# Hybrid mLSTM and ConvFFN decoder layer: in the opening, the weight rows of the third to eighth row block are loaded into slots of their own, in two parts

## The chip, the core and the metric

The kernel runs on one core of one Trainium2 chip. The metric is device time in microseconds (us) for one execution; less is better. A kernel is run several times and the median is given. One more execution is recorded by the hardware profiler, and the views quoted below come from it. PE is the matrix engine (TensorE), DVE is VectorE, ACT is ScalarE, POOL is GpSimd, and SP is SyncE, which here only issues loads and stores. "SPq" and "ACTq" are instructions that issue transfers on the queues of SP and ACT.

## The reference: what is computed

One decoder layer in float32, for 512 positions of 1024 channels. A vector `c` makes six modulation vectors through one matrix, `ada_w` (1024 x 6144). The input `x` is normalised, scaled and shifted with the first two of them, and goes through one wide projection. Of its columns, four groups feed four mLSTM heads; the last 2048 are the two halves of a gated unit (GLU), which goes on into a causal convolution of width 31. Cut to what the opening computes:

```python
cond = jax.nn.silu(c)
mod = cond @ ada_w[l] + ada_b[l]
sh1, sc1, g1, sh2, sc2, g2 = jnp.split(mod[:, None, :], N_MOD, axis=-1)
u = rms_norm(x, mix_pre_g[l]) * (1.0 + sc1) + sh1
proj = u @ w_in[l]
...
a, gt = jnp.split(glu, 2, axis=-1)
y = causal_dwconv(a * jax.nn.sigmoid(gt), cv_dw_w[l], cv_dw_b[l])
```

After this come the heads, an output projection, a residual, and a ConvFFN with its own modulation and residual. None of that is touched by the change.

## The kernel before, in words

**The layout.** Activations stand with channels on the 128 partitions and the 512 positions along the free axis. The 1024 channels are eight row blocks, k = 0 to 7. Float32 products are made as three reduced-precision products: each operand is split into a high part (a rounded copy, made on ACT, line 191) and a low part (operand minus high part, made on POOL, line 192), and PE forms high x high, high x low and low x high.

**The opening (lines 269 to 422).** Six column tiles of the GLU (`G0 = 6`) are accumulated at once in six banks, so that PE can work on one row block k as soon as that block of `u` is there. For each k the steps are:

- `w_rows(k)` (lines 341 to 343) loads 128 rows of 768 weight columns, 384 KB, on SP's queue. The tile comes from the pool `adas`, which has two buffers (`ADAS = 2`), so block k uses the buffer of block k - 2.
- `first_load(k)` (lines 241 to 246) loads 1 MB of `ada_w`, in two halves of 512 KB, on SP's queue. Four such buffers exist (two of `raws`, two of `early`), so block k + 4 uses the buffer of block k.
- `part_sum(k, i)` (line 330) multiplies each half with the broadcast `silu(c)` on DVE and sums it; `part_gains` (lines 335, 336) turns the two sums into a scale and a shift for each channel.
- `w_part(k, ...)` splits the weight rows into high and low parts, first 512 columns and then 256 (lines 191 and 192: two instructions on ACT, two on POOL).
- ACT writes the high part of `u` (line 405) and a full copy (line 406), POOL the low part (line 407; DVE for k = 7).
- PE does 18 products of 128 x 128 by 128 x 512 (line 350): six banks, three products each.

**The order.** SP and PE run their instructions in the order of the program text. In iteration k, SP is given `w_rows(k + 1)`, then `first_load(k + 2)`; iteration 0 has `w_rows(0)` and `first_load(1)` ahead of these, and iteration 2 has one more load, the rest of the small vectors (line 363). After the opening SP goes on with the 1 MB weight loads of the other GLU tiles (line 199 by way of `glu_weights`). On ACT, DVE and POOL the instructions of the opening keep the order of the text among themselves (`in_order`, lines 76 to 88). Other instructions of those three engines are placed between them by a planner, which gives an engine the ready instruction of the highest priority; a lower priority is marked by `tc.cur_priority += LATER`.

**A later user of the same two buffers.** `ada_block(i)` (lines 168 to 178) loads 512 KB of `ada_w` for the later modulation vectors into a tile of the same pool `adas`, with an issue on ACT's queue (line 174). The blocks 16 to 19 (lines 895 to 898) are the first of these and are marked `LATER`; they are multiplied with `cb` on DVE (line 176), about 230 us after the opening.

**Completion counters.** In the program as it is built, each load or store takes one of eight completion counters, by turns, whichever engine issues it, and its instruction waits on the issuing engine until the transfer eight places before it has landed.

**The pool `slots`** has 36 buffers of 128 x 512 float32 (`SLOTS = 36`). In the opening before, 20 are taken: 2 by `crow`, 8 by `xn`, 2 by `xjunks`, 8 by `xr`.

Of the kernel before, what the change touches and what calls it, by code (L numbers as in the profile page):

```python
# [10 lines left out]
F32 = mybir.dt.float32  # L11
# [6 lines left out]
P = 128  # L18
D = 1024
T = 512  # L20
# [35 lines left out]
def decoder_layer(ctx, tc, w_glu0, x, c, adaT, vecs, w_glu, w_qko, w_v0, w_vo, w_out, w_up, w_down, out):  # L56
    nc = tc.nc
# [9 lines left out]
    adas = ctx.enter_context(tc.tile_pool(name="adas", bufs=ADAS))  # L67
# [22 lines left out]
    def slot(name, dt=F32):  # L90
        return slots.tile([P, T], dt, tag="t", name=name)
# [93 lines left out]
    def w_split(src, name, pool=None, tag="w", eng=None):  # L185

        n = src.shape[1]
        pool = pool or wpool
        hi = pool.tile([P, T], F32R, tag=tag, name=f"{name}h")
        lo = pool.tile([P, T], F32R, tag=tag, name=f"{name}l")  # L190
        S.activation(hi[:, :n], src, AF.Copy)  # L191
        (eng or G).tensor_tensor(out=lo[:, :n], in0=src, in1=hi[:, :n].bitcast(F32), op=ALU.subtract)  # L192
        return hi, lo
# [108 lines left out]
    def u_tiles(name):  # L302
        hi = upool.tile([P, KT, T], F32R, tag="uh", name=f"{name}h")
        lo = upool.tile([P, KT, T], F32R, tag="ul", name=f"{name}l")
        return hi, lo, [(hi[:, j, :], lo[:, j, :]) for j in range(KT)]

    _, _, u = u_tiles("u")
# [8 lines left out]
    G0 = 6  # L316
# [22 lines left out]
    rows0 = {}  # L339

    def w_rows(k):
        rows0[k] = adas.tile([P, D], F32, tag="ada", name=f"wglu0_{k}")
        nc.sync.dma_start(rows0[k][:, : G0 * P], w_glu0[k])

    def w_part(k, a, n):
        wk.append(w_split(rows0[k][:, a : a + n], f"wglu0_{k}_{a}"))

    def glu_pass(ps, i, p):
        a, b = ((0, 0), (1, 0), (0, 1))[p]
# [2 lines left out]
    for k in range(KT):  # L352
        wk = []

        if k == 0:
            w_rows(0)
            first_load(1)
        if k + 1 < KT:
            w_rows(k + 1)
# [4 lines left out]
        hi, lo = u[k]  # L364
        if k == 0:
            w_part(k, 0, T)
            part_sum(k, 0)
            part_sum(k, 1)
# [6 lines left out]
            V.tensor_scalar(out=xr[0], in0=xT_ps[0], scalar1=sc, scalar2=sh, op0=ALU.mult, op1=ALU.add)  # L375
            G.tensor_tensor(out=lo, in0=xr[k], in1=hi.bitcast(F32), op=ALU.subtract)
            w_part(k, T, (G0 - 4) * P)
            x_out(4, V)
            x_out(5, S)
            for i, p in ((0, 0), (1, 0), (0, 1), (1, 1), (2, 0), (2, 1), (3, 0), (3, 1)):  # L380
                glu_pass(banks0[i], i, p)
            for j in range(6, KT):
                for tt in range(NT):
                    turn_x(j, tt)
            wk, first_wk = [], wk
            w_part(1, 0, T)
            wk, next_wk = first_wk, wk
            x_out(6, S)
# [6 lines left out]
        else:  # L395
            if k == 1:
                wk = next_wk
# [690 lines left out]
    def conv3(ps, i, name):  # L1088
        t = cvtile(f"{name}c")
        w = lambda tap: vcol("ffn_conv_w", tap * 44 + i)  # L1090
        S.activation(t, ps, AF.Identity, bias=vcol("ffn_conv_b", i), scale=w(2))
        for d in range(1, 3):
            V.scalar_tensor_tensor(out=t[:, d:], in0=ps[:, : T - d], scalar=w(2 - d), in1=t[:, d:], op0=ALU.mult, op1=ALU.add)
        return t
# [39 lines left out]
    for i in range(NF):  # L1134
# [21 lines left out]
        a = conv3(pa, i, f"fa{i}")  # L1156
# [222 lines left out]
```

## Time and profile before

| | us |
|---|---|
| median of 3 runs | 768.84 |
| lowest and highest of them | 767.8 and 769.19 |
| the profiled execution, its own time | 769.16 |
| its span | 767.4 |
| PE busy in that span | 756.0 (99%) |
| the opening's last product on PE begins | 50.79 |

The profiled execution is 0.32 above the median, and 1.8 of its time lies outside the span. In the views, the first number of a timeline row is the start in us from the start of the span and the second is the duration; a row's bracket at the end gives the idle time of the engine before it and what ended that idle time. Consecutive instructions of one kind are merged into one row with their count (x4). "wglu" is the weight rows, "ada" the modulation weights, "uh" and "ul" the two parts of `u`; the index of the block is left out, and is found by counting. PE is never at a granted clock below 1.00 in the stage that the change touches, and its products come every 0.23 us when nothing holds them.

### The profile page before, as it was taken

Reading aid. Unit: us, or ns where it says so; the run is one execution under the profiler, and the core shown is the slowest. Engines: PE = TensorE matmul, PEld = TensorE weight load, DVE = VectorE, ACT = ScalarE, POOL = GpSimd, SP = SyncE. Lnnn points to the kernel's source line nnn. Section 1 sums busy time; section 2 is a strip of 40 time slices with the busy share of each in tenths; the row PEclk is TensorE's granted clock in tenths of the full one; section 3 lists DMA queues with packets and bytes.
Section 4 is the critical chain, followed back from the end, with each engine's and each line's share of the span. In section 5 each row is a group of like instructions: output and inputs, shape, how many; then the busy total and the mean of one; then the engine's idle time right before and its main releaser. Section 6 shows DMA issues by size and latency. Waiting matters only on the chain.

```text
span 767.4 us, 10129 instructions
## 1 busy us (share of the span) xinstructions
PE 756.0 (99%) x3480; PEld 625.1 (81%) x3480; DVE 576.6 (75%) x837; ACT 410.7 (54%) x778; POOL 516.5 (67%) x428
## 2 busy tenths in 40 slices
PE   7999999999999999999999999999999999999996
PEld 5778898878788788888889988888888888888885
DVE  6669999979979696476989978675684775654547
ACT  6675428585665655573345444443534444566633
POOL 4779849796494872645631179786887884599943
PEclk9999999999999999999999999999999999999999
DMA  8973313411131241655965755666767565796273
GB/s 317 349 281 113 112 56 117 158 56 56 55 111 56 98 168 64 235 199 168 365 222 183 271 210 191 240 219 247 262 231 275 187 239 185 271 397 241 93 249 135
DMA packets 40136, 147.32 MB, mean 192 GB/s; under 512 B 3826, under 2 KB 5266, under 8 KB 30484
## 3 DMA queue, kind: packets, MB, share of 16 engines
q1 hardware_dynamic: 27524, 96.59, 34.9%
q10 hardware_dynamic: 12560, 50.08, 18.3%
q8 instruction: 27, 0.44, 0.2%
q14 instruction: 25, 0.20, 0.1%
HBM read 126.59 MB, written 20.07 MB: 191 GB/s over the span
## 4 chain that ended last, share of the span: by engine, by line
PE 93%; DMA 4%; POOL 1%; ACT 1%; issue 0%; DVEq 0%; SPq 0%; DVE 0%; POOLq 0%; ACTq 0%
PE up L210 31%; PE dn L210 13%; PE qko L210 13%; PE vo L210 9%; PE glu L210 7%; PE mixa L210 6%; PE mixb L210 6%; DMA wglu<-in_w_glu 3%; PE o L562 2%; PE s L551 2%; PE v L210 2%; PE glu L350 1%; DMA xn<-in_x 1%; PE xT L992 0%; PE hT L593 0%
## 5 line engine op out<-in xcount | busy, mean ns | idle before, releaser
L774 DVE SCALAR_TENSOR_TENSOR cv<-gt,cvw,cv 128x485 f32<-128x485 f32 (+24 forms) x200 | 137.2, 731 | 2.1 <-ACT cv L762 0.8
L770 POOL TENSOR_TENSOR cs<-cs,cs 128x510 f32<-128x510 f32 (+3 forms) x32 | 42.1, 1316 | 0.2
L192 POOL TENSOR_TENSOR wup_0l<-wup,wup_0h 128x512 fp32r<-128x512 f32 x18 | 25.0, 1389 | 19.4 <-ACT wup_0h L191 19.3
L210 PE MATMUL up<-u2h,wup_0h 128*128 128x512 f32 (+1 forms) x96 | 35.8, 373 | 0.0
L210 PE MATMUL up<-u2h,wup_0l 128*128 128x512 f32 (+1 forms) x96 | 35.7, 371 | 0.0
L210 PE MATMUL up<-u2h,wup_512h 128*128 128x512 f32 (+1 forms) x96 | 35.6, 371 | 0.0
L210 PE MATMUL up<-u2l,wup_512h 128*128 128x512 f32 (+1 forms) x96 | 35.6, 371 | 0.0
L210 PE MATMUL up<-u2h,wup_512l 128*128 128x512 f32 (+1 forms) x96 | 35.6, 371 | 0.0
L210 PE MATMUL up<-u2l,wup_0h 128*128 128x512 f32 (+1 forms) x96 | 35.6, 371 | 0.0
L210 PE MATMUL up<-u2h,wup_1024h 128*128 128x512 f32 (+1 forms) x92 | 35.0, 381 | 0.0
L210 PE MATMUL up<-u2l,wup_1024h 128*128 128x512 f32 (+1 forms) x92 | 34.9, 380 | 0.0
L210 PE MATMUL up<-u2h,wup_1536l 128*128 128x512 f32 (+1 forms) x92 | 34.9, 380 | 0.0
L210 PE MATMUL up<-u2h,wup_1536h 128*128 128x512 f32 (+1 forms) x92 | 34.9, 380 | 0.0
L210 PE MATMUL up<-u2l,wup_1536h 128*128 128x512 f32 (+1 forms) x92 | 34.9, 380 | 0.0
L210 PE MATMUL up<-u2h,wup_1024l 128*128 128x512 f32 (+1 forms) x92 | 34.9, 380 | 0.0
L176 DVE SCALAR_TENSOR_TENSOR junk<-ada,cb 128x1024 bf16<-128x1024 f32 x20 | 29.9, 1493 | 2.6 <-DMA ada<-in_adaT 2.5
L768 ACT ACTIVATE cs<-gt,cvw 128x511 f32<-128x511 f32 (+4 forms) x40 | 27.1, 713 | 6.1 <-POOL cs L770 3.5
L192 POOL TENSOR_TENSOR wup_1536l<-wup,wup_1536h 128x512 fp32r<-128x512 f32 x18 | 24.6, 1365 | 6.0 <-ACT wup_1536h L191 5.4
L191 ACT ACTIVATE wup_512h<-wup 128x512 fp32r<-128x512 f32 x22 | 13.8, 629 | 25.7 <-PE up L210 20.9
L192 POOL TENSOR_TENSOR wup_1024l<-wup,wup_1024h 128x512 fp32r<-128x512 f32 x18 | 23.6, 1314 | 5.0 <-ACT wup_1024h L191 5.0
L330 DVE SCALAR_TENSOR_TENSOR junk<-ada,cps 128x1024 bf16<-128x1024 f32 x16 | 19.5, 1220 | 9.8 <-DMA ada<-in_adaT 9.2
L1113 DVE TENSOR_TENSOR b<-b 128x512 f32<-128x512 f32 x11 | 19.4, 1762 | 8.6 <-POOL b L1112 8.6
(1097 smaller groups left out, 2726.8 us busy)
## 6 DMA issues: line engine op xcount, KB each, us to landing
wup<-in_w_up SPq DMA_DIRECT2D x22, 1024.0 KB, 5.0
b<-in_w_down ACTq DMA_DIRECT2D x11, 1024.0 KB, 5.1
spill_t<-b ACTq DMA_DIRECT2D x11, 1024.0 KB, 3.9
ada<-in_adaT ACTq DMA_DIRECT2D x20, 512.0 KB, 4.8
wqko<-in_w_qko SPq DMA_DIRECT2D x9, 1024.0 KB, 4.8
ada<-in_adaT SPq DMA_DIRECT2D x16, 512.0 KB, 7.5
wo<-in_w_out SPq DMA_DIRECT2D x8, 1024.0 KB, 5.5
wvo<-in_w_vo SPq DMA_DIRECT2D x6, 1024.0 KB, 4.8
```

Of the source, the lines that this page charges most:

```text
L176: t = V.scalar_tensor_tensor(out=junk, in0=r, scalar=1.0, in1=cb, op0=ALU.mult, op1=ALU.mult, accum_out=mod[:, i : i + 1])
L191: S.activation(hi[:, :n], src, AF.Copy)
L192: (eng or G).tensor_tensor(out=lo[:, :n], in0=src, in1=hi[:, :n].bitcast(F32), op=ALU.subtract)
L210: PE.matmul(ps, l, r, start=start and i == 0, stop=stop and i == 2, skip_group_check=again)
L330: V.scalar_tensor_tensor(out=junk, in0=first[k][:, i * D : (i + 1) * D], scalar=1.0, in1=cps, op0=ALU.mult, op1=ALU.mult, accum_out=part[: ...
L350: PE.matmul(ps, blk(wk, i)[a], u[k][b], start=k == 0 and p == 0, stop=k == KT - 1 and p == 1)
L551: PE.matmul(sp[:, :n], ks[d][:, cc * P : (cc + 1) * P], qs[d][:, cc * P :], start=d == 0, stop=d == 1)
L562: PE.matmul(o[:, : DH + 2], E[h][cc][:, a : a + P], vs[h][cc], start=cc == 0, stop=cc == tt)
L768: S.activation(t[:, d:], cvx[j][:, : T - d], AF.Copy, scale=w(CK - 1 - d))
L770: G.tensor_tensor(out=side[:, d:], in0=side[:, d:], in1=t[:, d:], op=ALU.add)
L774: tap = V.scalar_tensor_tensor(out=cp[:, d:], in0=cvx[j][:, : T - d], scalar=w(CK - 1 - d), in1=cp[:, d:], op0=ALU.mult, op1=ALU.add)
L1113: V.tensor_tensor(out=b22, in0=b22, in1=b11, op=ALU.subtract)
```

## The change

For k = 0 and 1 nothing changes but how the two parts are named. For k = 2 to 7, the 768 columns go into two tiles of the pool `slots`, the first 512 columns into one and the other 256 into another, with one load for each. There is no tile of `adas` for these blocks any more. The split reads the part instead of a column range of one tile.

```diff
     def w_rows(k):
-        rows0[k] = adas.tile([P, D], F32, tag="ada", name=f"wglu0_{k}")
-        nc.sync.dma_start(rows0[k][:, : G0 * P], w_glu0[k])
+        if k < 2:
+            t = adas.tile([P, D], F32, tag="ada", name=f"wglu0_{k}")
+            nc.sync.dma_start(t[:, : G0 * P], w_glu0[k])
+            rows0[k] = t[:, :T], t[:, T : G0 * P]
+        else:
+            rows0[k] = slot(f"wglu0_{k}a"), slot(f"wglu0_{k}b")[:, : G0 * P - T]
+            for z, a in zip(rows0[k], (0, T)):
+                nc.sync.dma_start(z, w_glu0[k][:, a : a + z.shape[1]])
 
     def w_part(k, a, n):
-        wk.append(w_split(rows0[k][:, a : a + n], f"wglu0_{k}_{a}"))
+        wk.append(w_split(rows0[k][a // T], f"wglu0_{k}_{a}"))
```

Twelve tiles of `slots` and six more loads on SP's queue come of it; the bytes are the same, and the order of the loads in SP's text is the same.

## The prediction

> **What bounds the kernel now.** I read the page first, then PE's waits, then PE's own rows around the change.
>
> ```profile
> span 767.4 us, 10129 instructions
> PE 756.0 (99%) x3480; PEld 625.1 (81%) x3480; DVE 576.6 (75%) x837; ACT 410.7 (54%) x778; POOL 516.5 (67%) x428
> PE cps L159 <- ACT crow L158: 2.9, 1, 2.9
> PE glu L350 <- ACT uh L371: 1.3, 1, 1.3
> PE glu L350 <- ACT uh L405: 0.9, 1, 0.9
> ```
>
> PE is busy 99% of the span. The last three rows are all the waits of PE that the trace lists (total us, times, longest): nothing after the opening waits. So a product that starts earlier at the end of the opening should end the kernel earlier, and the change can give back only what PE loses in the opening from block 2 on. Those losses are in PE's rows; each row is the first group of a block (k = 1 to 7), the last one the first product behind the opening.
>
> ```profile
> 20.67 1.07 PE L350 MATMUL glu<-uh,wglu_0h 128*128 128x512 f32 x4
> 24.75 1.07 PE L350 MATMUL glu<-uh,wglu_0h 128*128 128x512 f32 x4
> 29.02 1.21 PE L350 MATMUL glu<-uh,wglu_0h 128*128 128x512 f32 x4
> 33.29 1.21 PE L350 MATMUL glu<-uh,wglu_0h 128*128 128x512 f32 x4
> 37.54 1.07 PE L350 MATMUL glu<-uh,wglu_0h 128*128 128x512 f32 x4
> 42.72 1.20 PE L350 MATMUL glu<-uh,wglu_0h 128*128 128x512 f32 x4 [0.94 <-ACT uh L405]
> 46.94 1.07 PE L350 MATMUL glu<-uh,wglu_0h 128*128 128x512 f32 x4
> 51.02 0.39 PE L210 MATMUL glu<-uh,wglu_0h 128*128 128x512 f32 x1
> ```
>
> Block 1 takes 24.75 - 20.67 = 4.08 us and shows no gap. Seven such blocks from 20.67 would end at 20.67 + 7 x 4.08 = 49.23; they end at 51.02. **The whole prize is 1.79 us**: 0.19 on blocks 2 and 3 each (4.27 - 4.08), 0.17 on block 4, 1.10 on block 5 (5.18 - 4.08), 0.14 on block 6.
>
> What ends these gaps is in ACT's rows: the start of the weight split of blocks 3, 4 and 6, with ACT's idle time before it.
>
> ```profile
> 27.32 0.63 ACT L191 ACTIVATE wglu_0h<-wglu 128x512 fp32r<-128x512 f32 x1 [3.03 <-DMA wglu<-in_w_glu]
> 31.59 0.63 ACT L191 ACTIVATE wglu_0h<-wglu 128x512 fp32r<-128x512 f32 x1 [1.77 <-DMA wglu<-in_w_glu]
> 41.03 0.63 ACT L191 ACTIVATE wglu_0h<-wglu 128x512 fp32r<-128x512 f32 x1 [3.41 <-DMA wglu<-in_w_glu]
> ```
>
> Each is followed by its block on PE 1.7 us later (27.32 to 29.02, 31.59 to 33.29, 41.03 to 42.72): two splits, then the high part of `u`, in ACT's fixed order. So the landing of the weight rows sets these blocks. Why they land late is in SP's rows and waits.
>
> ```profile
> 9.46 2.27 SPq L245 DMA_DIRECT2D ada<-in_adaT  x2
> 18.18 0.33 SPq L343 DMA_DIRECT2D wglu<-in_w_glu  x1
> SPq L343 <- POOL wglu_512l L192: 14.5, 6, 4.3
> SPq L245 <- DMA ada<-in_adaT: 1.3, 1, 1.3
> ```
>
> SP issues nothing from 11.73 to 18.18, and waits 14.5 us in six places for POOL's last split, which frees the `adas` buffer. The last row is the completion counters: the second half of the third `ada` block waits for the first half of the first, eight transfers before.
>
> The transfers themselves:
>
> ```profile
> 0.00:18.00 18.00, 13.84 (x62) 10.05 (x63) 11.09 (x31) 12.34 (x24) 8.25 (x21) 1.00 0.86 320
> 10.00:18.00 8.00, 6.69 (x45) 5.80 (x44) 6.67 (x14) 5.69 (x10) 4.30 (x6) 1.00 1.02 404
> 18.00:22.00 4.00, 4.00 (x21) 3.38 (x20) 3.96 (x10) 3.13 (x7) 2.99 (x4) 1.00 0.88 265
> 22.00:36.00 14.00, 13.97 (x61) 10.96 (x60) 8.39 (x19) 8.07 (x15) 10.36 (x11) 1.00 1.02 376
> 36.00:42.00 6.00, 5.78 (x26) 4.46 (x24) 3.04 (x8) 2.56 (x6) 3.27 (x4) 1.00 0.92 299
> 0.00:25.00 25.00, 20.84 (x95) 15.89 (x96) 16.38 (x42) 17.74 (x33) 14.19 (x27) 1.00 0.88 319
> 0.00:27.30 27.30, 23.14 (x105) 17.80 (x106) 17.92 (x46) 17.74 (x33) 14.94 (x27) 1.00 0.89 325
> ```
>
> The last two columns are the busy share of the transfer engines and GB/s. They run at 376 to 404 when fed, with dips to 265 and 299: the change can fill only these dips.
>
> **The change part by part.** *The removed waits.* SP no longer waits for POOL from block 2 on. Its next limits are the counters and the four `ada` buffers. By 18 us SP should have issued block 2's rows, `ada` 3 and block 3's rows, and the queue stays full. I place the landings by bytes, with these sizes:
>
> ```profile
> ada<-in_adaT SPq DMA_DIRECT2D x16, 512.0 KB, 7.5
> wglu<-in_w_glu SPq DMA_DIRECT2D x8, 384.0 KB, 6.7
> xn<-in_x SPq DMA_DIRECT2D x4, 256.0 KB, 4.3
> vec<-in_vecs SPq DMA_DIRECT2D x1, 296.0 KB
> ```
>
> At 18 us 320 x 18 = 5.76 MB have moved; `x` (eight of 256 KB, 2.10), `ada` 0 to 2 (3.15), two row blocks (0.79) and the first vectors (0.03) are 6.06, so 0.30 MB of `ada` 2 is left. Behind it, at 390 GB/s (the middle of 376 and 404), block 3's rows have moved at 18.0 + (0.30 + 0.39 + 1.05 + 0.39)/0.39 = 23.5, block 4's (with 1.05 of `ada` 4 and 0.30 of vectors) at 27.9, and then 1.44 MB or 3.7 us for each: 31.6, 35.4, 39.1. A landing lags behind this count: at 25.01 DVE begins on the second half of `ada` 3 when 319 x 25 = 7.98 MB have moved and 7.50 were needed (0.48 MB, 1.2 us), and at 27.32 ACT begins block 3's rows with 8.87 moved and 7.89 needed (0.98 MB, 2.5 us). So the lag is 1.2 to 2.5 us, I take 1.85. Block 3 lands at 25.4, its products could begin at 27.1, and PE is free at 24.75 + 4.08 = 28.83. Block 6: 37.2, 38.9, needed at 41.07. Block 7: 41.0, 42.7, needed at 45.15. The second landing that a block needs, its `ada`, is 0.39 MB ahead of the rows, and DVE needs 1.22 + 0.08 + 0.47 us behind it:
>
> ```profile
> L330 DVE SCALAR_TENSOR_TENSOR junk<-ada,cps 128x1024 bf16<-128x1024 f32 x11 | 13.4, 1222 | 8.9 <-DMA ada<-in_adaT 8.4
> ```
>
> that, too, is before PE asks. **So far: -1.79 us.**
>
> *Six more issues and smaller pieces.* 0.33 us each on SP, which has 14.5 us of waits to hide them; without that cover 6 x 0.33 = 2.0. How the transfer engines take a part of 256 columns, 1 KB a partition, no row of the opening shows. Lower end 0; upper end the spread of the fed rates above, 376 against 404, 7% of 2.4 MB, 0.4 us. Both lie inside the 1.7 us by which blocks 3 to 7 land early. I take 0.
>
> *Twelve tiles of `slots`.* 20 + 12 = 32 of 36, so none waits in the opening; the later users come when all twelve are read. 0.
>
> *The two buffers that become free.* This is the term that speaks against the change. The next users of `adas` are the `LATER` loads of `ada_block` 16 and 17.
>
> ```profile
> 42.70 0.81 ACT L406 ACTIVATE xr<-xr,gsk 128x512 f32<-128x512 f32 x1
> 43.01 0.74 POOL L192 TENSOR_TENSOR wglu_512l<-wglu,wglu_512h 128x256 fp32r<-128x256 f32 x1
> 43.79 0.33 ACTq L174 DMA_DIRECT2D ada<-in_adaT  x1
> 19.60 0.74 POOL L192 TENSOR_TENSOR wglu_512l<-wglu,wglu_512h 128x256 fp32r<-128x256 f32 x1 [0.20 <-ACT wglu_512h L191]
> ```
>
> Before, the first is issued at 43.79, 0.04 after POOL's split of block 6 frees the buffer (43.01 + 0.74), in the middle of ACT's opening work: the planner puts it as early as a buffer allows. After the change the buffers are free when block 0's and block 1's rows are split, by 18.18 (SP's row above waited for the first) and at 19.60 + 0.74 = 20.34, and nothing else takes them. So I expect 2 x 0.52 = 1.05 MB, not needed for 200 us, to enter the opening at 18 to 24 us on ACT's queue, between the transfers that PE waits for: 1.05/0.39 = 2.7 us. Block 3 then lands at 23.5 + 2.7 + 1.85 = 28.05, its products begin at 29.75 instead of 29.02; block 4 lands at 32.45, begins at 34.15 (PE would be free at 33.83); block 5 lands at 36.15, and from here PE asks later than the rows come: 34.15 + 4 x 4.08 = 50.47, against 51.02: **-0.55**. With the lag of 1.2 block 4 begins at 33.5, -1.2; with 2.5 at 34.8, +0.1; at 376 instead of 390 GB/s block 4 is 4.9 MB on and 0.5 later, +0.6.
>
> *ACT's queue.* The two issues also hold ACT, by the same counters: each waits until the transfer eight places before has landed. By the nearest row the hold is 0.28 (ACT is done at 42.70 + 0.81 = 43.51 and issues at 43.79), twice at most; by the far end it is a rival below. ACT has 4.08 - (0.63 + 0.40 + 0.80 + 0.82) = 1.4 us idle in a block, so most of it is hidden:
>
> ```profile
> 27.86 0.40 ACT L191 ACTIVATE wglu_512h<-wglu 128x256 fp32r<-128x256 f32 x1
> 28.17 0.80 ACT L405 ACTIVATE uh<-xr,gsk 128x512 fp32r<-128x512 f32 x1
> 29.00 0.82 ACT L406 ACTIVATE xr<-xr,gsk 128x512 f32<-128x512 f32 x1
> ```
>
> I take 0.15 on the path. **Sum: -0.55 + 0.15 = -0.4 us.** The profiled execution (769.16, span 767.4) lies 0.32 above the median; the difference is taken from the median, 768.84 - 0.4 = 768.4.
>
> The Trainium skill, "DMA: Bandwidth & Descriptors", section "Queues, rings and completion order", says that each transfer engine goes round the queues that have work and changes after a packet. By that rule the two loads on ACT's queue take half of each engine while they last, however much SP has queued, which is the delay of 2.7 us used above; if they stood behind SP's queue instead, the sum would be -1.8. No row here decides it: I found none where a load on ACT's queue had a long queue of SP's beside it.
>
> **The rivals.** *The full prize, 768.84 - 1.8 = 767.0.* The two loads come late, or the lag is short and they hide. For it: a slack of 1.7 us at block 3 without them. Against it: the 0.04 us of the row at 43.79.
>
> *ACT held, slower: about 770.3.*
>
> ```profile
> 20.27 0.82 ACT L406 ACTIVATE xr<-xr,gsk 128x512 f32<-128x512 f32 x1
> ```
>
> With the queue full, eight transfers are always on their way, and an ACT issue placed after block 1's work (ACT ends it at 20.27 + 0.82 = 21.1) waits for transfers that land at 24 to 27 us (`ada` 3 and block 3's rows, by the count above, with and without the 2.7). Behind it in ACT's order stand block 2's splits and its `u`; PE waits for them, and POOL for ACT. Block 2 then begins at 24.4 + 0.33 + 1.7 = 26.4 at the least and 29 at the most, not 24.75; from there PE needs 6 x 4.08 = 24.5 us, so the opening ends at 50.9 to 53.5: -0.1 to +2.5, middle +1.2, and with POOL's queue behind it I say +1.5. It decides from a hold of about 1.8 us (26.55 + 24.5 = 51.02). For it: 8 transfers are only about 2.8 MB, 7 us of work. Against it: ACT may issue while it waits for rows anyhow (the 3.03 and 1.77 us of idle time above).
>
> *Another order elsewhere.* The planner may place later work of DVE, ACT and POOL differently; PE has no listed wait there that could shrink, so this can only cost, some tenths: 769.
>
> **How the numbers follow.** Forecast 0.53, full prize 0.22, ACT held 0.20, another order 0.05. What a measurement of this kernel tells from no change is about 0.2%, 1.5 us. Faster by more: 0.7 of the full prize (its spread is -1.2 to -1.9) and 0.07 of the forecast, 0.15 + 0.04, and 0.02 for a gain that I don't see: 0.21. Slower by more: half of ACT held and 0.06 of the others: 0.14. Within: 0.65. The forecast's own range is -1.2 to +0.6, 767.6 to 769.4. The 8-in-10 range takes in the full prize, 766.9, and ACT held up to 770.2.
>
> **What would show it.** SP's rows for the weight rows of block 2 at 12 to 14 us, not 18.18; no wait of SP for POOL's split in the opening; two rows of ACT's queue for `ada` at 18 to 25 us, not from 43.79 on; the first product behind the opening (51.02 before) at 50.6, at 49.2 for the full prize, and past 51.5 for ACT held, with ACT idle before block 2's split. The gap of 1.10 us behind block 5 should be gone in either of the first two cases. Wrong is all of it if the time behind the opening changes by more than the opening does.

## The result, and the profile after

The changed kernel takes 770.3 us (median, 768.56 to 772.63) and the kernel before, on the same chip, 768.39 us (767.57 to 770.17). The ratio is 1.002, 95% interval 1.0014 to 1.0026: slower by about 1.5 us by the ratio and by 1.9 us by the medians, where no change was forecast. A few executions of these kernels took far longer than all others (up to 4382 us); the ratios leave them out, and one of them, at 1555.59 us, was the execution first profiled for the experiment e5_bytes_on_sp. The page of the kernel after begins so:

```profile
span 768.6 us, 10144 instructions
```

The difference lies in the opening. PE's rows in the timeline of the kernel after, the first group of each block (k = 1 to 6; block 7's is left out) and the first product behind the opening:

```profile
20.32 1.07 PE L356 MATMUL glu<-uh,wglu_0h 128*128 128x512 f32 x4
24.40 1.07 PE L356 MATMUL glu<-uh,wglu_0h 128*128 128x512 f32 x4
29.11 1.19 PE L356 MATMUL glu<-uh,wglu_0h 128*128 128x512 f32 x4 [0.47 <-ACT uh L411]
34.96 1.21 PE L356 MATMUL glu<-uh,wglu_0h 128*128 128x512 f32 x4 [1.46 <-ACT uh L411]
39.91 1.20 PE L356 MATMUL glu<-uh,wglu_0h 128*128 128x512 f32 x4 [0.54 <-ACT uh L411]
44.13 1.07 PE L356 MATMUL glu<-uh,wglu_0h 128*128 128x512 f32 x4
...
52.29 0.39 PE L210 MATMUL glu<-uh,wglu_0h 128*128 128x512 f32 x1
```

From block 1 to the first product behind the opening PE takes 52.29 - 20.32 = 31.97 us; before it took 51.02 - 20.67 = 30.35. What lies behind is the same: 768.6 - 52.29 = 716.3 us, before 767.4 - 51.02 = 716.4. The gap of 1.10 us behind block 5 is gone (44.13 - 39.91 = 4.22), and new ones stand before blocks 3, 4 and 5: 0.63, 1.77 and 0.87 us over the 4.08 of a block.

SP's own rows of the timeline, and its longest wait (total us, times, longest):

```profile
12.60 0.33 SPq L349 DMA_DIRECT2D wglu_2a<-in_w_glu  x1
...
18.31 0.33 SPq L349 DMA_DIRECT2D wglu_3a<-in_w_glu  x1
19.59 0.33 SPq L349 DMA_DIRECT2D wglu_3b<-in_w_glu  x1
26.14 0.80 SPq L245 DMA_DIRECT2D ada<-in_adaT  x2
...
28.66 0.90 SPq L245 DMA_DIRECT2D ada<-in_adaT  x2
SPq L245 <- DMA ada<-in_adaT: 13.1, 7, 6.1
```

SP never waits for POOL's split now. But between 19.92 and 26.14 it issues nothing: one wait of 6.1 us ahead of `ada` 4. ACT's rows:

```profile
17.86 0.33 ACTq L174 DMA_DIRECT2D ada<-in_adaT  x1
20.04 0.33 ACTq L174 DMA_DIRECT2D ada<-in_adaT  x1
...
27.12 0.63 ACT L191 ACTIVATE wglu_0h<-wglu_3a 128x512 fp32r<-128x512 f32 x1 [3.65 <-DMA wglu_3a<-in_w_glu]
...
33.13 0.63 ACT L191 ACTIVATE wglu_0h<-wglu_4a 128x512 fp32r<-128x512 f32 x1 [3.22 <-DMA wglu_4a<-in_w_glu]
```

The two loads of `ada_block` 16 and 17 went out at 17.86 and 20.04, and ACT was not held: its issues slip in between its other work. What it then waits for is weight rows. The windows of the kernel after (last two columns: busy share of the transfer engines, GB/s) show SP's queue running dry behind its wait (in 22 to 24 us they still moved 405 GB/s):

```profile
24.00:26.00 2.00, 2.00 (x11) 1.65 (x10) 1.54 (x4) 0.00 (x0) 1.33 (x2) 1.00 0.90 344
26.00:28.00 2.00, 2.00 (x10) 1.68 (x9) 0.00 (x0) 0.69 (x2) 0.17 (x1) 1.00 0.44 120
```

The chain that ended last, followed back from 54 us, names what SP waited for:

```profile
17.86 8.20 DMA ada<-in_adaT
...
26.08 0.02 SPq L245
...
29.12 8.25 DMA ada<-in_adaT
```

It is the load that **ACT** issued at 17.86. SP's first half of `ada` 4 is the transfer eight places behind it in the program's order (between them stand two parts each of the rows of blocks 2 and 3, the two halves of `ada` 3, and the second early load), so both use the same completion counter, and SP's issue waits until `ada_block` 16, which nobody needs for 200 us, has landed 8.20 us after its issue. By then SP is late with everything: it issues `ada` 4, the vectors, block 4's rows, `ada` 5 and block 5's rows in 4.4 us (26.14 to 30.57), and the second half of `ada` 5, issued at 29.12, lands only 8.25 us later and sets block 5.

### The profile page after: what moved, and what is told of

It is laid out like the page before. It is cut to its first block, busy times and chain, and to the rows that moved or that the text cites. A ratio compares the mean times of both kernels' runs of the same rounds, so it can differ in the third digit from the quotient of the medians.

```text
span 768.6 us, 10144 instructions
## 1 busy us (share of the span) xinstructions
PE 755.7 (98%) x3480; PEld 624.9 (81%) x3480; DVE 578.5 (75%) x837; ACT 412.1 (54%) x778; POOL 517.9 (67%) x428
## 4 chain that ended last, share of the span: by engine, by line
PE 94%; DMA 4%; SPq 1%; issue 0%; ACT 0%; DVE 0%; DVEq 0%; POOLq 0%; POOL 0%; ACTq 0%
PE up L210 31%; PE dn L210 13%; PE qko L210 13%; PE vo L210 9%; PE glu L210 7%; PE mixa L210 6%; PE mixb L210 6%; PE o L568 2%; PE s L557 2%; DMA ada<-in_adaT 2%; PE glu L356 2%; PE v L210 1%; DMA wglu<-in_w_glu 1%; DMA xn<-in_x 1%; PE hT L599 0%; PE xT L998 0%
## 5 line engine op out<-in xcount | busy, mean ns | idle before, releaser
L191 ACT ACTIVATE wup_512h<-wup 128x512 fp32r<-128x512 f32 x22 | 13.8, 629 | 26.7 <-PE up L210 20.2
```

## The experiments

My theory after this: the early loads cost in two ways, by holding SP through the counter and by their own 1.05 MB. The rivals: that the bytes alone do it; that loading in two parts, or from slots, does it; that ACT is held. All ratios are against the kernel before, with 95% intervals. "Opening" is the time from block 1's first product to the first product behind the opening; seven blocks without a gap are 7 x 4.08 = 28.56 us.

**The change without its early loads (e1_pin).** The two loads are put back behind the end of the opening on ACT, everything else is as changed (`behind_ins` keeps an instruction behind another one on the same engine):

```diff
-        nc.scalar.dma_start(r, adaT[i // 2][...])
+        load = nc.scalar.dma_start(r, adaT[i // 2][...])
+        if i < 18:
+            behind_ins(load, opened[0])
...
-    S.activation(cb, cps, AF.Copy)
+    opened.append(S.activation(cb, cps, AF.Copy))
```

> The changed kernel, with the loads of ada_block 16 and 17 queued on ACT behind the copy that ends the opening, so that they can't enter it. Theory (the loss comes from these two loads: the first takes a completion counter, lands after 8.2 us, and SP's issue of ada 4 waits for it until 26.14): without them SP isn't held, the first product behind the opening comes at 49.2 to 49.8 instead of 52.29, and the time is 1.2 to 1.8 us below the kernel before (ratio 0.9977 to 0.9984). Rival (the six more loads use up the eight counters, so that SP runs dry anyway): SP still shows a wait of several us for an ada landing, the first product at 51 or later, ratio 1.000 to 1.002. Rival (another order of later work): the opening is as in the theory, and the total doesn't follow it.

767.49 us, ratio 0.9992 (0.9983 to 1.0). SP's row of `ada` 4 and PE's first and last rows of the opening:

```profile
18.28 1.55 SPq L251 DMA_DIRECT2D ada<-in_adaT  x2
20.23 1.07 PE L362 MATMUL glu<-uh,wglu_0h 128*128 128x512 f32 x4
48.79 0.39 PE L216 MATMUL glu<-uh,wglu_0h 128*128 128x512 f32 x1
```

`ada` 4 goes out 7.86 us earlier. 2.65 of these were lost ahead of the long wait: block 3's second part leaves SP at 16.94 here and left it at 19.59 in the changed kernel, where the two early loads stand in two of the eight places. The transfers stay at 395 to 414 GB/s from 18 to 42 us, and the opening is 48.79 - 20.23 = 28.56 us: no gap at all. So all that the change loses, it loses by the two early loads; slots and two parts in themselves are no loss. The time gained less than I expected, 0.6 us by the ratio in place of 1.2 to 1.8, with an interval that reaches 1. And in this profile, at a mean granted clock of 0.949, the stretch behind the opening took 766.8 - 48.79 = 718.0 us, not 716.3.

**The same once more (e1_again)**, run beside e5 and the changed kernel's second measurement:

> e1_pin once more, for a second profile and a narrower interval. Theory: the opening without a gap on PE again, seven blocks of 4.08 us; the time behind the first product after the opening as in the kernels before and after, 716.3 to 716.5 us, where the first profile of e1_pin had 718.0 at a granted clock of 0.95; ratio to before 0.9985 to 0.9995. Rival (the pinned loads cost 1.6 us behind the opening): 718.0 again.

767.48 us, ratio 0.9986 (0.9978 to 0.9995). Again no gap, and behind the opening 767.6 - 51.33 = 716.3 us: the 718.0 belonged to that one execution, not to the loads put back. But in the profiled execution block 1 began 2.5 us later:

```profile
22.77 1.07 PE L362 MATMUL glu<-uh,wglu_0h 128*128 128x512 f32 x4
51.33 0.39 PE L216 MATMUL glu<-uh,wglu_0h 128*128 128x512 f32 x1
10.00:18.00 8.00, 5.62 (x34) 4.38 (x34) 6.86 (x14) 5.72 (x11) 4.56 (x6) 0.89 1.02 406
18.00:22.00 4.00, 4.00 (x20) 3.25 (x19) 3.93 (x9) 2.41 (x5) 2.31 (x4) 0.80 1.03 396
```

The granted clock (third number from the end) was 0.89 and 0.80 in these windows.

**The split alone (e2_split_only).** The kernel before, with the rows of blocks 2 to 7 loaded in two parts into the same buffers:

```diff
-        nc.sync.dma_start(rows0[k][:, : G0 * P], w_glu0[k])
+        for a, b in ((0, G0 * P),) if k < 2 else ((0, T), (T, G0 * P)):
+            nc.sync.dma_start(rows0[k][:, a:b], w_glu0[k][:, a:b])
```

> The kernel before, with only one part of the change: the rows of blocks 2 to 7 are loaded in two parts, but still into the two buffers by turns. Theory: SP is paced by the buffers, the six more issues hide in its waits for POOL, and the time is that of before within 0.3 us (ratio 0.9996 to 1.0004). Rival (the two parts cost counters): 0.5 to 1.5 us slower (1.0007 to 1.002), with waits of SP for ada landings in place of those for POOL.

768.42 us, ratio 1.0006 (0.9998 to 1.0015): no difference that this measures. The interval takes in both what I expected and values of the rival, so the time doesn't decide between them; e1, which has the same two parts and no gap, does. SP still waits 11.5 us for POOL:

```profile
SPq L344 <- POOL wglu_512l L192: 11.5, 6, 4.3
```

**The place in the order, without the bytes (e3_small_early).** As changed, but only the first 32 columns (16 KB) of each of the two loads go early; the rest follows behind the opening. The counters are taken as in the change.

```diff
-        nc.scalar.dma_start(r, adaT[i // 2][...])
+        cut = 32 if i < 18 else 0
+        if cut:
+            nc.scalar.dma_start(r[:, :cut], adaT[i // 2][...])
+        load = nc.scalar.dma_start(r[:, cut:], adaT[i // 2][...])
+        if i < 18:
+            behind_ins(load, opened[0])
...
```

> As the changed kernel, but of the loads of ada_block 16 and 17 only the first 32 columns (16 KB each) are loaded where the changed kernel has the whole, and the rest behind the opening: the same counters are taken at the same places of the order, without the 1 MB. Theory (it is the late landing of the big load on ACT's queue that holds SP): the small load lands 3 to 4 us after its issue, SP issues ada 4 by 22, and the time is that of e1_pin within 0.4 us. Rival (that any load of ACT stands in the row of counters is enough): SP is held as in the changed kernel, and the ratio to before is 1.001 to 1.002.

768.95 us, ratio 1.001 (1.0001 to 1.0019). From the timeline and the windows:

```profile
17.93 0.33 ACTq L180 DMA_DIRECT2D ada<-in_adaT  x1
18.39 0.33 SPq L358 DMA_DIRECT2D wglu_3a<-in_w_glu  x1
23.66 1.52 SPq L254 DMA_DIRECT2D ada<-in_adaT  x2
24.10 0.63 ACT L200 ACTIVATE wglu_0h<-wglu_3a 128x512 fp32r<-128x512 f32 x1 [0.58 <-DMA wglu_3a<-in_w_glu]
22.00:26.00 4.00, 4.00 (x19) 3.34 (x18) 2.77 (x6) 3.33 (x6) 4.00 (x5) 1.00 0.73 213
```

With 16 KB in place of 512 SP's `ada` 4 is still held until 23.66, 5.4 us later than in e1_pin, and the queue runs dry (213 GB/s). In the chain that ended last, ACT's load of 16 KB, from 17.93 on, is what SP's issue waited for: it lands 23.66 - 17.93 = 5.7 us after its issue, as long as the 256 KB that SP queued beside it (24.10 - 18.39 = 5.7). I had expected 3 to 4 us and the time of e1_pin; the rival's ratio came. So the hold needs the place, not the bytes; the bytes prolong the wait itself from 3.6 to 6.1 us, and the delay of `ada` 4 against e1_pin from 5.4 to 7.9. The opening here was 49.89 - 20.40 = 29.49 us, 0.93 over e1_pin, and by the medians the small loads cost 768.95 - 767.49 = 1.5 us against e1_pin, beside which they ran.

**The bytes, without the place (e5_bytes_on_sp).** As changed, with the two loads put into SP's own order, one behind `ada` 4 and the vectors, one behind `ada` 5 (there they take places in the round too, but ACT issues none of them):

```diff
...
+        if k in (2, 3):
+            i = 14 + k
+            ahead[i] = adas.tile([P, D], F32, tag="ada", name=f"ada_{i}")
+            nc.sync.dma_start(ahead[i], adaT[i // 2][...])
```

> The changed kernel, with the loads of ada_block 16 and 17 issued by SP in its own order, behind the vectors of block 2 and behind ada 5: the same 1.05 MB in the opening, but no load on ACT's queue. Theory (most of the loss is the late landing on ACT's queue under a counter that SP waits for, the bytes alone cost little): the transfers stay at about 400 GB/s, the opening ends up to 1 us later than in e1_pin, ratio to before 0.999 to 1.0005. Rival (the bytes are the loss): the opening ends 2.5 to 3.5 us later than in e1_pin, ratio 1.0015 to 1.0025.

768.04 us, ratio 0.9997 (0.9988 to 1.0007). Its profile is from one more execution:

> The kernel of e5_bytes_on_sp once more, for a profile with PE at its usual clock. If the bytes alone cost, as the times say (0.6 us over e1_pin): SP's ada 4 at 18.1, the queue at 395 to 405 GB/s through 18 to 40 us, and gaps of PE of some tenths before blocks 3 to 5, 1 us in all at most, with the opening from block 1's first product to the first behind block 7 at 28.6 to 29.6 us. If the loads stall something as in the changed kernel: a wait of SP over 5 us and an opening over 30.5.

767.74 us. ACT's start on block 4's rows, and the only gap for which the trace lists a wait of PE (0.67 us over the 4.08 of a block):

```profile
30.74 0.63 ACT L192 ACTIVATE wglu_0h<-wglu_4a 128x512 fp32r<-128x512 f32 x1 [4.20 <-DMA wglu_4a<-in_w_glu]
37.37 1.19 PE L357 MATMUL glu<-uh,wglu_0h 128*128 128x512 f32 x4 [0.49 <-ACT uh L416]
```

SP is on time (`ada` 4 at 18.38), the queue stays at 388 to 409 GB/s, and the opening is 49.75 - 20.37 = 29.38 us, 0.82 over e1_pin. The 1.05 MB alone cost that much in the trace and 768.04 - 767.48 = 0.56 us by the medians, against e1_again, beside which they ran, though the intervals of the two ratios overlap.

**The two loads on ACT's queue, at another place in the order (e7_behind_block2).** They stand behind block 2's `xr`:

```diff
-        nc.scalar.dma_start(r, adaT[i // 2][...])
+        load = nc.scalar.dma_start(r, adaT[i // 2][...])
+        if i in (16, 17):
+            behind_ins(load, opened[2])
...
-            S.activation(xr[k], xr[k], AF.Identity, scale=sc, bias=sh)
+            opened[k] = S.activation(xr[k], xr[k], AF.Identity, scale=sc, bias=sh)
```

> The changed kernel, with the two loads of ada_block 16 and 17 queued on ACT behind block 2's xr (which ends at about 23.4 us in e1_pin) in place of 17.9 and 20.0 us; nothing else moved. The place in the round of eight counters moves with them: now SP's issues of block 6's rows (29.34 in e1_pin) and of ada 7 (31.05) come eight places behind the two loads and have to wait for their landings. Theory 'the order of issue decides': SP's ada 4 goes out at 18.3 us, as in e1_pin; the two loads land some 5.7 to 8.2 us after 23.5, at 29.2 to 32; block 6's rows leave SP at up to 32, 2.7 late, but PE asks for block 6 only at 40.6, so that delay is hidden. What is left is the transfer of the 1.05 MB itself (e5_bytes_on_sp: 0.6 us over e1_pin): 767.5 to 768.3, 1.5 to 2.5 below the changed kernel, and not one wait of SP longer than 3 us before 28 us. Rival 'early bytes cost wherever they stand in the opening': 769.3 or more, near the changed kernel. Rival 'ACT held' (of the prediction): ACT waits at its issue for block 3's rows and ada 3 to land, block 3's split starts a microsecond or more late (23.80 in e1_pin), PE has a gap before block 3 or 4, 768.5 to 769.5.

769.17 us, ratio 1.0013 (1.0004 to 1.0021): above what my theory gave (767.5 to 768.3), just below what its first rival gave (769.3), and inside what the second, *ACT held*, gave (768.5 to 769.5). From the timeline:

```profile
23.27 1.99 ACTq L178 DMA_DIRECT2D ada<-in_adaT  x2
25.31 0.63 ACT L197 ACTIVATE wglu_0h<-wglu_3a 128x512 fp32r<-128x512 f32 x1 [1.81 <-issue]
32.06 0.63 ACT L197 ACTIVATE wglu_0h<-wglu_4a 128x512 fp32r<-128x512 f32 x1 [4.25 <-DMA wglu_4a<-in_w_glu]
33.75 1.19 PE L362 MATMUL glu<-uh,wglu_0h 128*128 128x512 f32 x4 [0.99 <-ACT uh L417]
```

SP's `ada` 4 is on time (18.37), as the theory had it, and the queue stays full (394 to 403 GB/s from 24 to 30 us). But the two loads now come between block 4's rows and their transfer. ACT began these rows at 29.35 in e1_pin, at 30.74 in e5_again and at 32.06 here. With 0.39 MB per us, one load of 0.52 MB ahead of them is 1.34 us and two are 2.69: 1.39 and 2.71 were measured. In e1_pin block 4 had 1.4 us to spare (29.35 + 1.7 = 31.05, and PE began it at 32.47); here PE waits 1.15 us for it (33.75 - 28.52 - 4.08). ACT, too, is held here, 1.81 us of idle time at its own issues, and block 3's split comes 1.5 us later than in e1_pin (23.80), hidden behind PE's work on block 2. So the signs that the second rival named are all there (the hold, the late split, a gap before block 4), but its cause isn't: ACT was free again 4.25 us before it could begin block 4, and waited for these rows. The opening is 50.72 - 20.36 = 30.36 us, 1.80 over e1_pin. Behind it the profile has 767.9 - 50.72 = 717.2 us in place of 716.3, of which 0.6 is one wait of PE between 120 and 140 us that no other profile has. So what my theory had left out is that a load on the second queue takes transfer time from rows that are already queued on the first: the order of issue alone doesn't decide.

**The same aim without free buffers (e4_sides).** The kernel before, with the rows of blocks 2 to 5 loaded by one transfer each into the halves of two `side` tiles and those of 6 and 7 in `adas`. So nobody becomes free to load early:

```diff
-        rows0[k] = adas.tile([P, D], F32, tag="ada", name=f"wglu0_{k}")
+        if 2 <= k < 6:
+            if k % 2 == 0:
+                wide0.append(side(f"wglu0_{k}"))
+            rows0[k] = wide0[-1][:, k % 2 * D : (k % 2 + 1) * D]
+        else:
+            rows0[k] = adas.tile([P, D], F32, tag="ada", name=f"wglu0_{k}")
```

> The kernel before, with the rows of blocks 2 to 5 each by one load into halves of the two wide side buffers, which nothing uses until the opening ends, and blocks 6 and 7 in the two buffers of before: no wait for POOL, no load in two parts, and the two buffers don't come free before 43 us, so ada_block 16 and 17 stay behind. Theory: as e1_pin, 1.2 to 1.8 us below before (ratio 0.9977 to 0.9984), within 0.3 us of e1_pin. Rival (the parts cost counters): clearly better than e1_pin, by over 0.5 us. Rival (the prize isn't there): 1.000.

767.34 us, ratio 0.9989 (0.9981 to 0.9998): 0.85 us below the kernel before by the ratio, where 1.2 to 1.8 were expected. The loads of `ada_block` 16 and 17 stay where they were, and there is no gap:

```profile
21.89 1.07 PE L355 MATMUL glu<-uh,wglu_0h 128*128 128x512 f32 x4
50.45 0.39 PE L210 MATMUL glu<-uh,wglu_0h 128*128 128x512 f32 x1
39.72 0.33 ACTq L174 DMA_DIRECT2D ada<-in_adaT  x1
```

50.45 - 21.89 = 28.56 us. It is, with e1, the fastest version found; both are a little faster than the kernel before.

**Both kernels again.** The changed kernel:

> The changed kernel once more, on the chip of e5. Theory (SP held by the counter of the first early load): SP again issues nothing for about 6 us before ada 4, at 26 us within 0.7, the first product behind the opening at 52.0 to 52.6, ratio to before 1.001 to 1.003. Rival (the hold was one execution's accident): the hold under 3 us in this one, the product before 51.

769.8 us, ratio 1.0016 (1.0007 to 1.0025). SP's `ada` 4 went out at 25.38, behind a wait of 5.2 us, with ACT's two loads at 19.01 and 21.56. Block 1 began late in this execution, and yet the opening ended where it had ended in the first profile of this kernel:

```profile
22.10 1.07 PE L356 MATMUL glu<-uh,wglu_0h 128*128 128x512 f32 x4
52.19 0.39 PE L210 MATMUL glu<-uh,wglu_0h 128*128 128x512 f32 x1
```

Counted from block 1 this opening is 52.19 - 22.10 = 30.09 us, no longer than those of the kernel before. For the time it is the end of the opening that counts: 52.29 and 52.19 here, 50.43 to 51.02 in three profiles of the kernel before.

The kernel before:

> The kernel before, a second profile of it. Theory: the profile that the prediction was worked from is of an execution about 1 us slower than the median, and the 1.10 us on PE behind block 5 is its own: here the opening from block 1 takes 29.2 to 29.8 us instead of 30.35. Rival: 30.2 to 30.5 again, and the gap behind block 5 with it.

> The kernel before once more, to see how long its opening usually is: from block 1's first product to the first behind block 7 it took 30.35 us in the execution shown and 29.90 in before_again; gap-free it is 28.56. If 30.35 is usual, 30.2 to 30.5 again and a gap of about 1.1 behind block 5; if the execution shown was a slow one, 29.4 to 30.0 and that gap 0.7 or less.

768.58 and 768.89 us, with openings of 29.90 us (20.53 to 50.43) and 30.56 us (20.20 to 50.76). In the last, the gap behind block 5 is again 42.45 - 37.30 - 4.08 = 1.07 us:

```profile
37.30 1.07 PE L350 MATMUL glu<-uh,wglu_0h 128*128 128x512 f32 x4
42.45 1.20 PE L350 MATMUL glu<-uh,wglu_0h 128*128 128x512 f32 x4 [0.92 <-ACT uh L405]
```

So the opening shown before the change, 30.35 us, was not an unusually long one among the three, against what I had come to think.

## Why the prediction was wrong

The forecast was 768.4 us, in effect no change; the result is 770.3 us, a small loss, outside the stated range of 766.9 to 770.2. Step by step:

*The removed waits: right.* SP's block 2 rows went out at 12.60 us, and no wait for POOL's split is left.

*The whole prize of 1.79 us: right in the trace, too large in the time.* Three profiles of the kernel before show openings 1.3 to 2.0 us longer than the gap-free 28.56, and e1 and e4 take all of that away. Yet by the ratios they are only 0.6 and 1.1 us (e1, twice) and 0.85 us (e4) below the kernel before. A part of the reason: with no gap left, the end of the opening moves with block 1's start one for one (20.23 to 48.79 and 22.77 to 51.33 in e1), while where transfers set the end it doesn't move (20.32 to 52.29 and 22.10 to 52.19 in the changed kernel). An execution with a late block 1, at a lower granted clock, thus takes the prize away. No profile of the kernel before shows such an execution, but the recorded runs, each with its mean granted clock, fit: at 0.995 and 0.996 those of e1 and e4 (7 of 33, median 768.8) are 0.3 us below those of the kernel before beside them (7 of 60, 769.1), and above that 1.0 us (767.2 against 768.1). Even there it is 1.0 and not 1.79, and why stays open. One estimate: in ten of the twelve profiles the time is 718.0 to 718.15 us more than the end of the opening, and by that the median executions of the kernel before (768.1 to 768.6 in four rounds of runs) ended it at about 50.0 to 50.5 us, where the three profiles have 50.43, 50.76 and 51.02: two of the three profiled openings ended later than is usual.

*More issues, smaller pieces, twelve slots: right at 0.* e1 has all of them and no gap; e2 can't be told from no change.

*The two buffers that become free: the mechanism was right, and one of its sizes by luck.* I expected the loads at 18 to 24 us; they came at 17.86 and 20.04. Block 3's rows were expected to land at 28.05 and were taken at 27.12; e3, which issues them at the same time but has the small loads, takes them at 24.10, so the large ones delayed them by 3.0 us, against the 2.7 worked out. Block 4's were expected at 32.45 and taken at 33.13, but that is luck: SP issued them at 27.49, and the prediction had no such delay. e7 shows the 2.7 us of delay by bytes almost alone, as worked out, and the cost of 1.24 us put on it (from -1.79 to -0.55) lies between e5's 0.82 and e7's 1.80 in the opening.

*The step that failed is "the queue stays full".* I placed all of SP's issues by bytes, and the sum has no term for a hold of SP by the early loads. Already block 3's rows left SP at 18.31 and 19.59, not by 18; then SP was held at `ada` 4 until 26.14 by the counter that ACT's load had taken, the transfer engines fell to 120 GB/s, and the opening came to its end at 52.29, not at 50.6. Over the gap-free opening the early loads were to cost 1.24 us; in the first profile they cost 31.97 - 28.56 = 3.41 (in the second, where block 1 began 1.8 us later and the end was the same, 1.53). The bytes alone (e5) cost 0.82 and the places, with 16 KB each, 0.93 (e3): in the first profile both together, with the place held until the large load has landed, cost more than their sum. I had the rule in the text (an issue waits for the transfer eight places before, whichever engine issued it), and applied it to ACT alone, under "ACT's queue": there I asked what holds ACT's two issues and not whose issues stand eight places behind them. The answer needs nothing beyond the order in the program: `ada` 4 and `ada` 5. Had I asked, the landing would have been to estimate, and the trace of before has a row for it, though the prediction says that it found none: the load that ACT issued at 43.79 stood beside a full queue of SP's (q1, 97.1% of the transfer engines' time in 43 to 47 us) and landed 6.8 us after its issue:

```profile
q1 hardware_dynamic: 233, 1.63, 97.1%
...
ada<-in_adaT ACTq DMA_DIRECT2D x1, 512.0 KB, 6.8
```

An issue at 18 us and a landing of 6.8 would have put `ada` 4 at 24.8 us; with the 8.20 that came it went out at 26.14.

*ACT's queue, +0.15: wrong in place.* ACT was not held at all in the changed kernel; the rival *ACT held* forecast 770.3 us, which is the time that came, but by another engine's wait, so it was not borne out. Its signs (ACT idle before block 2's split) are absent: block 2 began at 24.40, with no gap. e7 shows that a hold of ACT of 1.81 us at such an issue is possible and can be hidden.

*The Trainium skill's rule, "DMA: Bandwidth & Descriptors", section "Queues, rings and completion order"* (each engine goes round the queues that have work): in the kernel after, SP's queue (q1) and ACT's (q10) moved, in 18 to 20, 20 to 22 and 22 to 24 us (packets, MB, share of the engines):

```profile
q1 hardware_dynamic: 397, 0.78, 104.7%
...
q1 hardware_dynamic: 187, 0.69, 87.0%
q10 hardware_dynamic: 30, 0.12, 15.3%
...
q10 hardware_dynamic: 125, 0.45, 57.2%
q1 hardware_dynamic: 132, 0.34, 43.4%
```

In the last of these windows both have work, and they move about as many packets each, as the rule says. But ACT's load, issued at 17.86, moves nothing until 21.2 us, and only at 26.06 has it landed: the start and the end are outside the rule as I used it, and 8.20 us is three times what half of 0.39 MB per us gives for 0.52 MB (2.7 us).

*Behind the opening: right.* 716.3 us against 716.4.

## What to carry to other kernels

When a change frees a buffer, find who takes it next and where that new transfer falls in the order of all transfers: with completion counters taken by turns, it delays its own engine's neighbours and also the issue that comes eight places behind it, here on another engine. A load that nobody needs yet should be tied to a place behind the work that is short of transfers (e1), or the buffer should not become free (e4). And read the size of a prize from more than one execution, and ask what else moves the point from which it is counted.

## What the runs showed of the hardware that I had not expected

- A load on ACT's queue beside a full queue of SP's starts late and lands late: after the issue no packet of it moved for 3.3 us in the changed kernel (17.86 to 21.2), 3.6 in e3 (17.93 to 21.5) and 3.4 in e7 (23.27 to 26.7), and 16 KB landed after 5.7 us, 512 KB after 8.2. The Trainium skill, "DMA: Bandwidth & Descriptors", section "Queues, rings and completion order", states that the write that counts a completion lands only after all earlier writes of its transfer engine, across queues. The 5.7 us of the 16 KB, equal to those of SP's 256 KB beside it, would agree with that, but 3.6 of them are the late start, and no run here shows what the other 2.1 are.
- A load on the second queue does take bandwidth from rows that were queued earlier on the first: in e7 rows issued 2.6 us before ACT's loads (20.64 against 23.27) were delayed by 2.7 us against e1_pin.
- The granted clock in the first 22 us differs between executions of one kernel (0.96 and 0.95 in e1_pin against 0.89 and 0.80 in e1_again), and block 1 began at 20.23 or 22.77 us.
